# Broadcasting the decay rows of a state-space mixer: row layout in DRAM and the queue that loads them

## The chip, the cores and the metric

The kernel runs on one core of a Trainium2 chip. The metric is the device time of one execution in microseconds; the program is launched once and there is nothing to overlap it with. The engines are named as in the profile: PE (matrix multiplication), PEld (its weight loads), DVE (vector), ACT (scalar), POOL (GpSimd) and SP (the engine that does nothing here but issue DMAs). A DMA that SP or ACT issues goes through that engine's hardware queue; one that POOL issues goes through the software queue.

## The reference

One layer of a streaming encoder over 512 tokens of width 2048. A modulated RMS norm feeds one input projection, whose columns are split between two mixers; their outputs are projected, added to the input, and followed by a gated feed-forward with a short convolution. The change touches the second mixer only, the state-space one (four groups of four heads, chunks of tokens):

```python
dt = softplus(dt_raw + dt_bias)
a_head = -exp(a_log)
acum = cumsum(dt * a_head, within a chunk)            # one number per head and token
seg = exp(where(t >= s, acum[t] - acum[s], -inf))     # decay from token s to token t
cb = einsum('bctgn,bcsgn->bcgts', cm, bm)
y_diag = einsum('bcgts,bcgrts,bcsgrp->bctgrp', cb, seg, xdt)
```

For `seg` every partition (a token s) needs the whole row `acum[t]` of its head: a row of 512 numbers copied to all 128 partitions.

## The kernel before, in words

The weights stream through in chunks. `wchunk` has SP load two blocks of 128 rows into a `raw` tile (five buffers, shared with the tiles `m` of the modulation weights), ACT casts it to a high part `whi` (L161) and DVE subtracts to get the low part `wlo` (L162), two buffers each; PE multiplies each pair three times (L166 to L168). This runs from the start of the kernel to its end. Between the big matmuls, PE takes small steps of the two mixers: they are Python generators, advanced one step after every third big matmul by `small`, at most two at a time. Their matmuls write the two `mis` banks, so the third group in line waits until DVE or ACT has read the first.

`ssd_dt` computes the running sums `acum` for all 16 heads and four token blocks with one matmul into 64 rows (block-major, head inside), copies them to the SBUF tile `acr` (L398) and stores them to the DRAM tile `acrow` (L399). `ssd_mix(g)` handles a group of four heads; the groups run in pairs, 0 and 3, then 2 and 1. Its helper `decay(h)` loads the row of one head into a tile `mm` on all partitions (L434, sixteen loads in the kernel), adds the negative sums of the partition's own token (`negb`, L437), clips at zero (L439), takes the exponential on ACT (L440) and multiplies by the masked `cb` (L441). PE then multiplies `mm` by `xdt` (L487), DVE adds the result to `y` (L492), and PE makes the part that comes from earlier chunks (L497), which DVE scales and adds (L499, L503). At the end of `decay`, DVE has used the row and ACT the exponential; the next head's row is loaded while this head's matmuls run.

The `mm` tiles come from the pool of nine 2 KB-per-partition tiles that `T` hands out, in turn with all other temporaries. A scheduler (the tile framework) fixes the order of each engine's instructions when the program is built, and puts in the waits: a load waits for the last reader of its buffer, and hardware-queue loads take turns on eight semaphores, so that each also waits for the load that had its semaphore before.

In the background, `mod_unit` computes the modulation of later stages: SP loads a tile `m` (512 KB) between two weight chunks and DVE adds it into `macc` with two multiply-adds (L189). In the stretch of the state-space mixer every other weight chunk is followed by such a load.

Of the kernel before, what the change touches and what calls it, by code (L numbers as in the profile page):

```python
# [7 lines left out]
F32 = mybir.dt.float32  # L8
# [6 lines left out]
P = 128  # L15
S = 512
# [18 lines left out]
def hybrid_block_kernel(  # L35
# [6 lines left out]
    nc = tc.nc  # L42
# [22 lines left out]
    def T(name="t", dtype=F32):  # L65
        return tmp.tile([P, 512], dtype, tag="t", name=nm(name))
# [10 lines left out]
    def MIS(name="mis"):  # L77
        return psm.tile([P, 512], F32, tag="mis", name=nm(name))
# [4 lines left out]
    def CT(shape, name, dtype=F32):  # L83
        return cst.tile(shape, dtype, tag=name, name=name)
# [3 lines left out]
    def bc(ap, shape):  # L88
        return ap.unsqueeze(len(ap.shape)).broadcast_to(shape)
# [263 lines left out]
        A.activation(out=xbc[g][:, which, :], in_=y, func=AF.Silu)  # L353

    drm = ctx.enter_context(tc.tile_pool(name="drm", bufs=1, space=bass.MemoryType.DRAM))
    acrow = drm.tile([64, P], F32, tag="acrow", name="acrow")
    dtt = CT([P, 64], "dtt")
    dta = CT([P, 64], "dta")
    negb = CT([P, 16, 4, 2], "negb")
# [2 lines left out]
    def ssd_dt(src):  # L362
        pt = MIS()
        for t in range(NT):
            PE.transpose(out=pt[:, t * P:(t + 1) * P], in_=src[:, t * P:(t + 1) * P], identity=ident)
        xb, e, z, z2, p = (T(s_)[:, 0:64] for s_ in ("xb", "en", "zz", "z2", "pp"))

        def c4(t_):
            return t_.rearrange("p (c h) -> p c h", c=4)

        V.tensor_tensor(out=c4(xb), in0=c4(pt)[:, :, 0:16], in1=dtb.unsqueeze(1).broadcast_to([P, 4, 16]), op=ALU.add)
        V.tensor_tensor(out=c4(xb), in0=c4(pt)[:, :, 64:80], in1=c4(xb), op=ALU.add)
        V.scalar_tensor_tensor(out=e, in0=xb, scalar=-1.0, in1=xb, op0=ALU.mult, op1=ALU.min)
        A.activation(out=e, in_=e, func=AF.Exp)
        V.tensor_scalar(out=z, in0=e, scalar1=2.0, scalar2=None, op0=ALU.add)
        V.reciprocal(out=z, in_=z)
        V.tensor_tensor(out=z, in0=z, in1=e, op=ALU.mult)
        V.tensor_tensor(out=z2, in0=z, in1=z, op=ALU.mult)
        V.tensor_scalar(out=p, in0=z2, scalar1=1.0 / 19, scalar2=None, op0=ALU.mult)
        for k in (17, 15, 13, 11, 9, 7, 5, 3):  # L380
            V.scalar_tensor_tensor(out=p, in0=p, scalar=1.0 / k, in1=z2, op0=ALU.add, op1=ALU.mult)
        V.scalar_tensor_tensor(out=p, in0=p, scalar=1.0, in1=z, op0=ALU.add, op1=ALU.mult)
        V.tensor_scalar(out=xb, in0=xb, scalar1=0.0, scalar2=None, op0=ALU.max)
        V.scalar_tensor_tensor(out=dtt, in0=p, scalar=2.0, in1=xb, op0=ALU.mult, op1=ALU.add)
        V.tensor_tensor(out=c4(dta), in0=c4(dtt), in1=an.unsqueeze(1).broadcast_to([P, 4, 16]), op=ALU.mult)
        pc = MIS()
        for i, m in enumerate((tri, suf, ones, tri64, l1m)):
            PE.matmul(out=pc[:, i * 64:(i + 1) * 64], lhsT=m, rhs=dta, start=True, stop=True)
        A.activation(out=e3.rearrange("p a b -> p (a b)"), in_=pc[:, 0:192], func=AF.Exp)
        V.tensor_scalar(out=negb[:, :, :, 0].rearrange("p h c -> p c h"),  # L390
                        in0=pc[:, 192:256].rearrange("p (c h) -> p c h", h=16),
                        scalar1=-1.0, scalar2=None, op0=ALU.mult)
        V.tensor_copy(out=negb[:, :, :, 1].rearrange("p h c -> p c h"),
                      in_=pc[:, 256:320].rearrange("p (c h) -> p c h", h=16))
        pr = MIS()
        PE.matmul(out=pr[0:64, 0:P], lhsT=dta, rhs=tri64, start=True, stop=True)
        ar = T("acr")
        V.tensor_copy(out=ar[0:64, 0:P], in_=pr[0:64, 0:P])  # L398
        nc.gpsimd.dma_start(out=acrow, in_=ar[0:64, 0:P])  # L399

    def ssd_mix(g):

# [28 lines left out]
        def decay(h):  # L431
            hh = 4 * g + h
            m = mt[h] = T("mm")
            nc.gpsimd.dma_start(out=m.rearrange("p (c t) -> p c t", c=4),  # L434
                                in_=acrow.rearrange("(c h) t -> h c t", h=16)[hh].partition_broadcast(P))
            m8 = m.rearrange("p (a t) -> p a t", a=8)
            V.tensor_tensor(out=m8, in0=m8, in1=bc(negb[:, hh, :, :].rearrange("p c b -> p (c b)"), [P, 8, 64]),  # L437
                            op=ALU.add)
            V.tensor_scalar(out=m, in0=m, scalar1=0.0, scalar2=None, op0=ALU.min)  # L439
            A.activation(out=m, in_=m, func=AF.Exp)  # L440
            V.tensor_tensor(out=m, in0=m, in1=cbm, op=ALU.mult)  # L441

        decay(0)
        for cp in range(2):
            ps = MIS()
            for cc in range(2):
                for b in range(2):
                    t = 2 * cp + cc
# [33 lines left out]
        for h in range(4):  # L482
            if h < 3:
                decay(h + 1)
            ps = MIS()
            for cch in range(4):
                PE.matmul(out=ps[:, cch * HD:(cch + 1) * HD], lhsT=mt[h][:, cch * P:(cch + 1) * P],  # L487
                          rhs=xdt[:, cch, h * HD:(h + 1) * HD], start=True, stop=True)
                yield 0
            for cp in range(2):  # L490
                yh = ycols(cp)[:, :, h * HD:(h + 1) * HD]
                V.tensor_tensor(out=yh, in0=yh, in1=ps[:, cp * 128:(cp + 1) * 128].rearrange("p (t f) -> p t f", t=2),  # L492
                                op=ALU.add)
            if h < 3:
                ps = MIS()
                cch = h + 1
                PE.matmul(out=ps[:, 0:256], lhsT=xb[:, 3, cch * P:(cch + 1) * P], rhs=hst[h], start=True, stop=True)  # L497
                t = T("yo")[:, 0:256]
                V.tensor_tensor(out=t.rearrange("p (h f) -> p h f", h=4),  # L499
                                in0=ps[:, 0:256].rearrange("p (h f) -> p h f", h=4),  # L500
                                in1=bc(eac[:, cch, hs], [P, 4, HD]), op=ALU.mult)
                yo = yv(cch)[:, g * 256:(g + 1) * 256]
                V.tensor_tensor(out=yo, in0=yo, in1=t, op=ALU.add)  # L503
                yield 0
# [215 lines left out]
    for st, k0, k1 in SEGMENTS:  # L720
# [44 lines left out]
        if k1 == KT and st == 2:  # L765
            ssd_dt(dtraw)
# [52 lines left out]
    for j in range(2):  # L819
# [5 lines left out]
        for t in range(NT):  # L825
            sg = T("gs")
            A.activation(out=sg, in_=accs[t], func=AF.Silu)
            for i in range(4):
                h = 4 * j + i
# [208 lines left out]
```

## Time and profile before

| what | value |
|---|---|
| median of 3 runs | 2513.89 us (2510.45 to 2513.9) |
| the profiled execution | 2516.08 us |
| its span, first to last instruction | 2514.4 us |
| granted PE clock, mean over the span | 0.988 |
| DVE, ACT, POOL busy | 60%, 30%, 2% |
| the sixteen loads `mm<-acrow` | 256 KB each, issued from 287.6 to 437.9 us |

The span is 1.7 us shorter than the execution that it belongs to, and that execution lies 2.2 us above the median. The modulation and the first weight chunks fill the time to some 250 us, the state-space mixer runs beside the projection from about 290 to 460 us, the other mixer up to about 850 us, the output projection to 1060 us, and the feed-forward takes the rest. Times in the views of the profile count from the first instruction. "Busy" of PE includes modelled ends of matmuls, so what matters is where it was idle, how long, and what ended the idle time, and how fast its clock ran (the column PEclk, 1.00 being full speed).

### The profile page before, as it was taken

The numbers are of one execution on the slowest core, as the hardware profiler recorded it, in microseconds if no ns is written. First come the engines' busy times: TensorE is split into PE (matmuls) and PEld (weight loads), VectorE is DVE, ScalarE is ACT, GpSimd is POOL, SyncE is SP. The second block draws the span as 40 slices with busy tenths as digits, with TensorE's granted clock in tenths as the row PEclk, the third lists the DMA queues.
The fourth block names the chain that finished last, engine by engine and source line by source line (L and its number), as shares of the span: only waits on it lengthen the run. The fifth ranks groups of instructions, "written<-read, shape, count | busy, mean of one in ns | idle before, by whom it ended". The sixth has DMA issues, their size and how long they took to land.

```text
span 2514.4 us, 29234 instructions
## 1 busy us (share of the span) xinstructions
PE 2443.9 (97%) x11287; PEld 2015.4 (80%) x11287; DVE 1497.7 (60%) x2253; ACT 754.8 (30%) x1035; POOL 54.1 (2%) x66
## 2 busy tenths in 40 slices
PE   6999998999999999999999999999999999999998
PEld 5777877788878777887888888888888888888887
DVE  6884866556767656587636363635454545454557
ACT  6323422221322432332222222222222222232323
POOL 4000000000000000000000000000000000000000
PEclk8999999999999999999999999999999999999999
DMA  8893575335455666466323332333323232323242
GB/s 272 263 280 107 113 125 106 96 109 151 144 159 155 235 198 200 140 203 230 98 95 98 95 101 93 100 94 99 97 96 101 92 101 93 101 93 100 96 130 85
DMA packets 262823, 335.87 MB, mean 134 GB/s; under 512 B 18092, under 2 KB 182524, under 8 KB 261404
## 3 DMA queue, kind: packets, MB, share of 16 engines
q1 hardware_dynamic: 260432, 327.42, 41.5%
q0 software_dynamic: 1568, 4.31, 2.3%
q10 hardware_dynamic: 684, 2.28, 0.3%
q8 instruction: 88, 1.44, 0.2%
q14 instruction: 51, 0.42, 0.0%
HBM read 329.72 MB, written 4.23 MB: 133 GB/s over the span
## 4 chain that ended last, share of the span: by engine, by line
PE 81%; DMA 9%; DVE 7%; ACT 2%; issue 1%; SPq 0%; POOL 0%; ACTq 0%; DVEq 0%; POOLq 0%
PE acc L166 26%; PE acc L168 25%; PE acc L167 25%; DMA m<-in_w_mod_dram 7%; DVE wlo L162 2%; PE mis L547 2%; DVE macc L189 1%; DVE macc L238 1%; DMA raw<-in_w_in_dram 1%; ACT whi L161 1%; DMA x<-in_x_dram 1%; DMA mm<-acrow 0%; PE mis L201 0%; PE mis L487 0%; POOL rstd L265 0%
## 5 line engine op out<-in xcount | busy, mean ns | idle before, releaser
L162 DVE TENSOR_TENSOR wlo<-raw,whi 128x1024 fp32r<-128x1024 f32 (+1 forms) x408 | 490.4, 1203 | 744.9 <-ACT whi L161 739.3
L161 ACT CAST whi<-raw 128x1024 fp32r<-128x1024 f32 (+2 forms) x416 | 424.3, 1021 | 1403.3 <-PE acc L167 596.5
L166 PE MATMUL acc<-hhi,whi 128*128 128x512 f32 x1920 | 770.0, 402 | 11.7 <-ACT whi L161 7.1
L168 PE MATMUL acc<-hhi,wlo 128*128 128x512 f32 x1920 | 751.6, 394 | 3.6 <-DVE wlo L162 3.4
L167 PE MATMUL acc<-hlo,whi 128*128 128x512 f32 x1920 | 753.0, 392 | 0.0
L166 PEld LDWEIGHTS acc<-hhi,whi 128*128 128x128 f32 x1920 | 362.9, 189 | 87.2 <-ACT whi L161 11.2
L168 PEld LDWEIGHTS acc<-hhi,wlo 128*128 128x128 f32 x1920 | 362.4, 189 | 83.1 <-DVE wlo L162 6.5
L167 PEld LDWEIGHTS acc<-hlo,whi 128*128 128x128 f32 x1920 | 363.3, 189 | 67.9 <-issue 0.2
L166 PE MATMUL acc<-whi,act 128*128 128x512 f32 x640 | 249.0, 389 | 0.0
L167 PE MATMUL acc<-wlo,act 128*128 128x512 f32 x640 | 249.0, 389 | 0.0
L168 PE MATMUL acc<-whi,act 128*128 128x512 f32 x640 | 249.0, 389 | 0.0
L189 DVE SCALAR_TENSOR_TENSOR macc<-m,cT,macc 128x512 f32<-128x512 f32 x240 | 179.9, 750 | 106.8 <-DMA m<-in_w_mod_dram 102.6
L166 PE MATMUL acc<-whi,hhi 128*128 128x512 f32 x384 | 168.6, 439 | 0.0
L168 PE MATMUL acc<-whi,hlo 128*128 128x512 f32 x384 | 154.8, 404 | 0.0
L167 PE MATMUL acc<-wlo,hhi 128*128 128x512 f32 x384 | 154.0, 401 | 0.0
L166 PEld LDWEIGHTS acc<-whi,act 128*128 128x128 f32 x640 | 120.1, 188 | 25.0
L168 PEld LDWEIGHTS acc<-whi,act 128*128 128x128 f32 x640 | 120.1, 188 | 25.0
L167 PEld LDWEIGHTS acc<-wlo,act 128*128 128x128 f32 x640 | 120.1, 188 | 24.9
L950 DVE TENSOR_TENSOR g<-acc,gate 128x512 f32<-128x512 f32 x160 | 105.2, 683 | 3.9
L166 PE MATMUL acc<-mhi,whi 128*128 128x512 f32 x256 | 105.2, 411 | 0.0
L547 PEld LDWEIGHTS mis<-q,FK 128*128 128x128 f32 x448 | 83.5, 191 | 27.1 <-issue 8.3
L951 DVE TENSOR_TENSOR x<-x,g 128x512 f32<-128x512 f32 x160 | 105.1, 682 | 0.0
(263 smaller groups left out, 2249.8 us busy)
## 6 DMA issues: line engine op xcount, KB each, us to landing
raw<-in_ffn_w_up_dram SPq DMA_DIRECT2D x352, 256.0 KB, 2.9
m<-in_w_mod_dram SPq DMA_DIRECT2D x128, 512.0 KB, 4.3
raw<-in_ffn_w_down_dram SPq DMA_DIRECT2D x88, 512.0 KB, 3.6
m<-in_w_mod_dram SPq DMA_DIRECT2D x128, 256.0 KB, 4.3
raw<-in_w_in_dram SPq DMA_DIRECT2D x96, 256.0 KB, 3.5
raw<-in_w_in_dram SPq DMA_DIRECT2D x48, 512.0 KB, 3.8
raw<-in_w_out_dram SPq DMA_DIRECT2D x32, 512.0 KB, 4.6
x<-in_x_dram SPq DMA_DIRECT2D x8, 1024.0 KB, 10.6
```

Source lines behind the costliest of these rows:

```text
L161: A.copy(out=h_, in_=r_)
L162: V.tensor_tensor(out=l_, in0=r_, in1=h_.bitcast(F32), op=ALU.subtract)
L166: PE.matmul(out=ps, lhsT=lh, rhs=rh, start=first, stop=False)
L167: PE.matmul(out=ps, lhsT=lh, rhs=rl, start=False, stop=False)
L168: PE.matmul(out=ps, lhsT=ll, rhs=rh, start=False, stop=last)
L189: V.scalar_tensor_tensor(out=acc, in0=last[:, k, :], scalar=cT[:, kt:kt + 1], in1=acc, op0=ALU.mult, op1=ALU.add)
L238: V.scalar_tensor_tensor(out=acc, in0=m[:, k, :], scalar=cT[:, kt:kt + 1], in1=acc, op0=ALU.mult, op1=ALU.add)
L547: PE.matmul(out=ps[:, cch * 64:(cch + 1) * 64], lhsT=k[:, cch * P:(cch + 1) * P], rhs=qv[:, cch * npc:(cch + 1) * npc, 1, :], start=True, ...
L950: V.tensor_tensor(out=m, in0=accs[t], in1=gates[5][:, cs], op=ALU.mult)
L951: V.tensor_tensor(out=x1[t][:, cs], in0=x1[t][:, cs], in1=m, op=ALU.add)
```

## The change

Three lines. The DRAM tile becomes one row of 512 numbers (2 KB) per head; the store (still POOL's) scatters the 64 rows of 512 bytes to their places; and each broadcast reads one contiguous row and is issued by ACT on its hardware queue rather than by POOL on the software queue.

```diff
-    acrow = drm.tile([64, P], F32, tag="acrow", name="acrow")
+    acrow = drm.tile([16, S], F32, tag="acrow", name="acrow")
...
-        nc.gpsimd.dma_start(out=acrow, in_=ar[0:64, 0:P])
+        nc.gpsimd.dma_start(out=acrow.rearrange("h (c t) -> c h t", c=4), in_=ar[0:64, 0:P])
...
-            nc.gpsimd.dma_start(out=m.rearrange("p (c t) -> p c t", c=4),
-                                in_=acrow.rearrange("(c h) t -> h c t", h=16)[hh].partition_broadcast(P))
+            nc.scalar.dma_start(out=m, in_=acrow[hh].partition_broadcast(P))
```

The changed file is a line shorter, so everything behind L434 has a number lower by one there (L437 is L436, and so on). SP's instructions stand in the same order as before. ACT gets sixteen more rows, POOL loses sixteen, and on DVE and PE the scheduler moves instructions of the mixer by a few places. Three such places follow; numbers behind a name tell buffers apart.

ACT where the first pair of groups begins: `cy` and `xbc` belong to the short convolution, `whi` is the cast of a weight chunk. Before:

```order
L353 ACTIVATE xbc_126<-cy_2423 128x512
L349 ACTIVATE cy_2430<-xbc_126,p_663 128x512
L161 CAST whi_2633<-raw_2632 128x1024
L353 ACTIVATE xbc_126<-cy_2430 128x512
L440 ACT_TABLE_LOAD
L440 ACTIVATE mm_2495<-mm_2495 128x512
```

and now:

```order
L353 ACTIVATE xbc_126<-cy_2423 128x512
L349 ACTIVATE cy_2430<-xbc_126,p_663 128x512
L434 DMA mm_2495<-acrow 128x512
L434 DMA mm_2508<-acrow 128x512
L434 DMA mm_2694<-acrow 128x512
L161 CAST whi_2633<-raw_2632 128x1024
L434 DMA mm_2707<-acrow 128x512
L353 ACTIVATE xbc_126<-cy_2430 128x512
```

The first four broadcasts stand behind the last-but-one step of the convolution, and three of them ahead of a weight cast.

ACT at the last pair's end, where `q` belongs to the other mixer's first heads. Before:

```order
L522 ACTIVATE q_3292<-acc_2871 128x512
L161 CAST whi_3434<-raw_3433 128x1024
L440 ACT_TABLE_LOAD
L440 ACTIVATE mm_3337<-mm_3337 128x512
L440 ACTIVATE mm_3348<-mm_3348 128x512
L161 CAST whi_3485<-raw_3484 128x1024
L440 ACTIVATE mm_3414<-mm_3414 128x512
L440 ACTIVATE mm_3425<-mm_3425 128x512
```

and now:

```order
L521 ACTIVATE q_3292<-acc_2871 128x512
L434 DMA mm_3337<-acrow 128x512
L434 DMA mm_3348<-acrow 128x512
L161 CAST whi_3434<-raw_3433 128x1024
L439 ACT_TABLE_LOAD
L439 ACTIVATE mm_3337<-mm_3337 128x512
L439 ACTIVATE mm_3348<-mm_3348 128x512
L434 DMA mm_3414<-acrow 128x512
L161 CAST whi_3485<-raw_3484 128x1024
L434 DMA mm_3425<-acrow 128x512
L439 ACTIVATE mm_3414<-mm_3414 128x512
L439 ACTIVATE mm_3425<-mm_3425 128x512
```

Both weight casts now stand behind broadcasts, and each of these four broadcasts waits, on ACT, for the last reader of its buffer: mm_3337 and mm_3414 for matmuls of L487, mm_3348 and mm_3425 for additions of L503.

DVE in the first pair, where `y` is what a `mis` bank is emptied into. Before:

```order
L189 SCALAR_TENSOR_TENSOR macc_2931<-m_3019,cT,macc_2931 128x512 x2
L437 TENSOR_TENSOR mm_2768<-mm_2768,negb 128x512
L437 TENSOR_TENSOR mm_2779<-mm_2779,negb 128x512
L162 TENSOR_TENSOR wlo_2874<-raw_2872,whi_2873 128x1024
L439 TENSOR_SCALAR mm_2768<-mm_2768 128x512
L439 TENSOR_SCALAR mm_2779<-mm_2779 128x512
L492 TENSOR_TENSOR y_2449<-y_2449,mis_2774 128x2x64
L492 TENSOR_TENSOR y_2450<-y_2450,mis_2774 128x2x64
```

and now:

```order
L189 SCALAR_TENSOR_TENSOR macc_2931<-m_3019,cT,macc_2931 128x512
L436 TENSOR_TENSOR mm_2768<-mm_2768,negb 128x512
L189 SCALAR_TENSOR_TENSOR macc_2931<-m_3019,cT,macc_2931 128x512
L438 TENSOR_SCALAR mm_2768<-mm_2768 128x512
L436 TENSOR_TENSOR mm_2779<-mm_2779,negb 128x512
L162 TENSOR_TENSOR wlo_2874<-raw_2872,whi_2873 128x1024
L440 TENSOR_TENSOR mm_2768<-mm_2768,cbm_2493 128x512
L438 TENSOR_SCALAR mm_2779<-mm_2779 128x512
L491 TENSOR_TENSOR y_2449<-y_2449,mis_2774 128x2x64
L491 TENSOR_TENSOR y_2450<-y_2450,mis_2774 128x2x64
```

One multiplication by the mask moved ahead of the two additions that empty the bank; on PE, the matmul that waits for this bank (L497 into mis_2822) moved behind three more big matmuls.

## The prediction

> **What bounds the kernel now.** I read the page's totals first, then the stretches, then what ended PE's idle time, then the chain of waits through those places.
>
> ```profile
> span 2514.4 us, 29234 instructions
> PE 2443.9 (97%) x11287; PEld 2015.4 (80%) x11287; DVE 1497.7 (60%) x2253; ACT 754.8 (30%) x1035; POOL 54.1 (2%) x66
> 260.00:330.00 70.00, 69.74 (x328) 57.06 (x327) 61.67 (x96) 33.68 (x45) 4.37 (x6) 1.00 0.58 116
> 330.00:460.00 130.00, 115.72 (x551) 94.51 (x550) 78.92 (x155) 31.96 (x41) 8.21 (x11) 0.93 0.59 112
> 460.00:590.00 130.00, 129.83 (x694) 108.61 (x694) 78.74 (x160) 29.67 (x54) 2.05 (x2) 1.00 0.38 110
> ```
>
> PE bounds the kernel. The last three rows are stretches: start and end, length, then busy time of PE, PEld, DVE, ACT and POOL, the granted PE clock, the DMA share and GB/s. Eleven of the sixteen broadcasts are issued in the middle one, and there alone PE is idle, 14.3 us of 130, and its clock falls to 0.93, 9 us lost at most. The stretch after it, with as much DVE work, loses nothing: that is the floor to be reached. POOL's 2% says that issuing costs it nothing that matters; what a broadcast does elsewhere is the question.
>
> ```profile
> PE mis L497 <- DVE y L492: 11.8, 3, 4.4
> PE mis L449 <- DVE cbm L427: 2.2, 1, 2.2
> 345.00 0.40 PE L168 MATMUL acc<-whi,hlo 128*128 128x512 f32 x1
> 349.27 0.67 PE L497 MATMUL mis<-xbc 128*128 128x256 f32 x2 [3.87 <-DVE y L492]
> 380.53 0.33 PE L449 MATMUL mis<-ident,xbc 128*128 128x128 f32 x1 [2.21 <-DVE cbm L427]
> 433.60 2.05 PE L497 MATMUL mis<-xbc 128*128 128x256 f32 x4 [4.37 <-DVE y L492]
> 448.77 0.89 PE L497 MATMUL mis<-xbc 128*128 128x256 f32 x2 [3.56 <-DVE y L492]
> ```
>
> So the 14.0 us are four gaps, and each ends when DVE has emptied a bank. Why is DVE late? The chain of waits (start, length, what):
>
> ```profile
> 335.58 8.57 DMA m<-in_w_mod_dram
> 344.18 0.76 DVE macc L189
> 345.63 1.29 DVE mm L437 x2
> 346.92 1.14 DVE wlo L162
> 348.06 0.67 DVE mm L439 x2
> 348.73 0.41 DVE y L492 x2
> 371.78 6.53 DMA m<-in_w_mod_dram
> 379.79 0.70 DVE cbm L427
> 419.33 9.16 DMA m<-in_w_mod_dram
> 437.94 8.63 DMA mm<-acrow
> ```
>
> Ahead of gaps 1 to 3 DVE stands in its queue at `macc`, waiting for a modulation tile that takes 6.5 to 9.2 us; behind it stand the weight split and the additions that PE needs. Gap 4 is a broadcast itself. The DMA view says how unusual this is; the first two rows are from 330 to 460 us, the next two from 480 to 730, the rest from the page.
>
> ```profile
> m<-in_w_mod_dram SPq DMA_DIRECT2D x7, 512.0 KB, 5.6
> mm<-acrow POOLq DMA_DIRECT2D x11, 256.0 KB, 9.2
> m<-in_w_mod_dram SPq DMA_DIRECT2D x34, 512.0 KB, 3.7
> raw<-in_w_in_dram SPq DMA_DIRECT2D x24, 256.0 KB, 3.4
> gate<-in_b_mod_dram ACTq DMA_DIRECT2D x1, 1024.0 KB, 4.7
> q0 software_dynamic: 1568, 4.31, 2.3%
> q10 hardware_dynamic: 684, 2.28, 0.3%
> ```
>
> The last column of the first five is the median from issue to landing. A modulation tile takes 3.7 us where no broadcast runs.
>
> **The change, part by part.**
>
> *One broadcast.* The page's queue rows (packets, MB, share of 16 engines' span) give the software queue 2.3% of 16 x 2514 us, 925 engine-us for 4.31 MB, or 54 for one broadcast: 3.4 us of all sixteen engines. ACT's hardware queue, whose bytes are mostly `gate`, also a broadcast to 128 partitions, took 121 for 2.28 MB: 13 for a broadcast, 0.8 us of all sixteen. From issue to landing the ends are 3.4 us (a plain load of 256 KB) and 9.2 (as now); I take 3.5, since `gate` moved four times the bytes by this queue in 4.7. Broadcasts of 2 KB rows are not in the trace, only `gate`'s of 8 KB; per byte they would have to cost four times as much to be where the software queue is.
>
> The Trainium skill speaks against this: its page "DMA: Bandwidth & Descriptors" (section "Issuing engines are not separate DMA queues") says that DMAs of ACT, SP and POOL run on the same 16 engines and interleave, and that another issuer saves only issue time. By it the modulation tiles would stay late; that is rival B, and the two queue rows, 54 against 13, speak against reading it so here.
>
> *Gap 1.* The tile issued at 335.58 now has two broadcasts just ahead of it (they stand behind the cast `whi` whose split frees this tile's buffer), so 3.7 + 2 x 0.8 = 5.3: it lands at 340.9. In DVE's new order come two `macc` (0.7 each), two L437 (0.6 each), one L439 (0.3), the split (1.14), one L441 (0.6 like L437), one L439 and two L492 (0.4 together): 5.4, so the bank is free at 346.3. PE used to run dry at 345.4; three big matmuls (0.4 each, overlapping) moved ahead of the waiting one make it 346.1. I leave 0.5 of 3.87, to be safe.
>
> *Gap 2.* No broadcast is in flight at 371.78 any more: the second pair's first four now stand behind the cast below. 3.7 rather than 6.53 us puts the bank 2.8 us earlier, more than the gap of 2.2. Nothing is left.
>
> *Gap 3.* 419.33 + 3.7 + 0.8 for the broadcast just ahead of it = 423.8; two `macc` 1.5, split 1.1, two L437 1.2, two L439 0.7, L492 0.4: 428.7, before PE ran dry at 429.2. Nothing left.
>
> *Gap 4.* The last broadcast went at 437.94, when L503 had freed its buffer. Without gap 3 (4.4) and the slow clock up to there (1.4) that is 432.1, and it lands at 435.6 to 436; L437, L441, L439 and L492 take 2, to 438. PE, earlier by gap 3 and all of its slow clock (4.4 + 2.6), would run dry at 445.2 - 7.0 = 438.2. I leave 0.3.
>
> *Clock.* The clock is the third column from the end; the stretch cut at the gaps reads:
>
> ```profile
> 330.00:370.00 40.00, 36.13 (x181) 30.08 (x180) 25.34 (x55) 9.73 (x14) 5.22 (x7) 0.96 0.76 119
> 370.00:410.00 40.00, 37.77 (x177) 29.64 (x175) 28.51 (x44) 10.22 (x13) 0.00 (x0) 0.96 0.41 112
> 410.00:450.00 40.00, 31.81 (x149) 26.37 (x150) 19.76 (x44) 9.02 (x12) 2.99 (x4) 0.90 0.66 105
> ```
>
> Gaps 1 and 2 each lose 0.04 x 40 = 1.6 us of clock, gap 3 up to 4.0, and the rest of the 9 (0.07 x 130 for the whole stretch) falls behind gap 4. Some of it lay in idle time, so I take 8.
>
> *ACT.* The timeline around the moved loads, and `gate`'s issue:
>
> ```profile
> 287.64 0.80 POOL L434 DMA_DIRECT2D mm<-acrow  x1 [25.96 <-ACT xbc L353]
> 307.92 0.82 ACT L349 ACTIVATE cy<-xbc,p 128x512 f32<-128x512 f32 x1
> 310.91 0.69 DVE L437 TENSOR_TENSOR mm<-mm,negb 128x512 f32<-128x512 f32 x1
> 376.29 1.05 ACT L161 CAST whi<-raw 128x1024 fp32r<-128x1024 f32 x1 [5.79 <-PE acc L167]
> 382.13 0.68 DVE L437 TENSOR_TENSOR mm<-mm,negb 128x512 f32<-128x512 f32 x1
> 421.06 0.75 POOL L434 DMA_DIRECT2D mm<-acrow  x1 [2.25 <-DVE y L503]
> 423.29 1.05 ACT L161 CAST whi<-raw 128x1024 fp32r<-128x1024 f32 x1 [6.18 <-PE acc L167]
> 1058.01 0.39 ACTq L257 DMA_DIRECT2D gate<-in_b_mod_dram  x1
> ```
>
> Sixteen issues of 0.39 each are 6 us of an engine that is 30% busy; what it costs is place. POOL issued the first at 287.6; on ACT it stands behind the L349 that starts at 307.92, so it goes at about 308.4 (the issue at 1058.01 ran beside an activation) and lands at 311.9, where DVE wants it at 310.91: a wait of 1.0, with the weight split and the mixer's `xdt` behind it, on the engine that is busy 61.7 of 70 us there. PE has no idle time there to hide it in, but a weight chunk in hand: 0 to 1.3, I take 0.7. The second pair's four go at 377.4, behind the cast of 376.29, and land from 380.9, before DVE's 382.13. The waits that ACT now makes are short: the one for L503 ended at 421.06 and the cast behind it is not ready before 423.29. SP's loads now also wait for broadcasts that had their semaphore before, but each of these goes some 9 us earlier or more.
>
> *The store* goes out in 64 pieces of 512 bytes rather than in one run; it had landed before POOL's first broadcast at 287.64, and its first reader now comes 20 us later: nothing. *POOL* loses sixteen issues that nothing waited for: nothing.
>
> *Sum.* Idle 14.0 - 0.8 = 13.2, clock 8, start -0.7: 20.5, say 20. The profiled execution took 2516.1 (its span 2514.4 and 1.7 around it), which gives 2496; it lay 2.2 above the median of the runs, so against that median, 2513.9, I forecast 2494.
>
> **Rivals.**
>
> A. Part of the gaps stays. Gap 1 and gap 4 close with nothing to spare above. If a broadcast ahead of a modulation tile costs it 2 us rather than 0.8, gaps 1 and 3 keep 2.0 and 1.5, each with its half-speed window (1.6 and 2.6): 0.5 is already left, so 7.2 less than 20 is won, 12.8, 2501. For it: DMA shares of 0.76 and 0.66 in two of the rows above, so that queues are long. Against it: 13 engine-us. The Trainium skill's "TensorE: Matmul & The Clock Gate" (section "What's actually happening") has the clock halve after an idle window of about 3.4 us; by that, such gaps would cost no clock, and A would be 2497. The trace differs: behind gap 2, 2.21 us, the clock fell to 0.96.
>
> B. The bytes are what holds the engines, and ACT's issuing changes only the landing. Then gaps 1 to 3 stay, gap 4 (3.6, and 1.6 of clock) goes, 0.7 is lost at the start: 4.5 won, 2509.
>
> C. Slower: reading one 2 KB row 128 times is what takes 9.2 us, in either layout and queue. Then the late issue bites: the first broadcast lands at 317.6, DVE stands 6.7 us at 310.91 and PE, with a chunk in hand but the `mis` banks behind DVE, loses about 6 and 2.5 of clock; the second pair's lands at 386.6, 4.5 after DVE wants it, of which 2 reach PE; gap 2 still goes (2.2 and 1.6). 10.5 lost less 3.8, 6.7: 2521. It decides from a landing of some 6 us on. Against it: `gate`.
>
> **How the numbers follow.** My forecast 0.62, A 0.20, B 0.08, C 0.06, and 0.04 for a loss elsewhere that eats the gain, 2509 to 2520. The forecast's own range is 2490 (all four gaps, 9 of clock, no loss at the start) to 2499. With A (2496 to 2505) and part of B, the range 2489 to 2508 leaves out C, the losses and most of B, 0.17. What this measurement can tell from no change is 0.2%, 5 us: faster than 2508.9 are the forecast, A and half of B, 0.86; within it the other half of B and half of the losses, 0.06; slower C and the other half, 0.08.
>
> **What would show it.** Right: `mm` landing in 3 to 4 us; `m` between 330 and 440 us near 4; the waits of L497 and L449 for DVE under 2 us in total; a PE clock of 1.00 there; POOL's queue with some 0.1% of the engines. Wrong in size: DVE waiting for `mm` at the start of a pair by more than 1.5 us (place on ACT), or `m` still above 5.5 (A, B). Wrong in kind: PE waiting for `whi`, which would mean that ACT stood at a broadcast with a weight cast behind it.

## The result, and the profile after

The changed kernel takes 2499.39 us, median of 4 runs (2497.71 to 2500.41), against 2513.89 (2510.45 to 2516.95) before: a ratio of 0.9942, with a 95% interval of 0.9925 to 0.9959. That is 14.5 us less; 20 were forecast. The time lies inside the forecast's range and on the forecast's side, 5.4 us above the 2494 that was forecast. The profiled execution took 2500.41.

First the page's totals, its rows of the two queues, and the first two stretches that were shown of before (the columns are the same).

```profile
span 2498.7 us, 29189 instructions
PE 2435.8 (97%) x11287; PEld 2008.5 (80%) x11287; DVE 1498.6 (60%) x2253; ACT 755.3 (30%) x1035; POOL 42.3 (2%) x50
q10 hardware_dynamic: 2988, 6.47, 0.9%
q0 software_dynamic: 304, 0.12, 0.0%
260.00:330.00 70.00, 68.18 (x322) 55.86 (x321) 59.47 (x91) 33.27 (x44) 0.68 (x1) 1.00 0.37 112
330.00:460.00 130.00, 126.70 (x642) 104.80 (x641) 88.21 (x169) 36.25 (x46) 0.00 (x0) 0.99 0.42 124
```

PE's idle time in the long stretch went from 14.3 to 3.3 us, and the clock from 0.93 to 0.99; in the stretch ahead of it, 1.6 us were lost. The DMA share fell from 0.59 to 0.42, although more bytes were moved (124 GB/s, 112 before). The rest of what was idle is in three gaps:

```profile
PE mis L448 <- DVE y L455: 4.0, 2, 2.4
PE mis L496 <- DVE y L491: 0.7, 1, 0.7
317.48 0.63 PE L448 MATMUL mis<-ident,xbc 128*128 128x128 f32 x4 [1.55 <-DVE y L455]
348.88 0.67 PE L496 MATMUL mis<-xbc 128*128 128x256 f32 x2 [0.72 <-DVE y L491]
387.42 0.41 PE L448 MATMUL mis<-ident,xbc 128*128 128x128 f32 x2 [2.43 <-DVE y L455]
```

The gap at 349 is what is left of gap 1. Those at 317 and 387 are new: they stand where a pair of groups begins. The loads and the chain of waits through these places say why:

```profile
m<-in_w_mod_dram SPq DMA_DIRECT2D x8, 512.0 KB, 3.7
mm<-acrow ACTq DMA_DIRECT2D x12, 256.0 KB, 4.7
309.31 4.55 DMA mm<-acrow
337.67 5.63 DMA m<-in_w_mod_dram
375.31 8.31 DMA mm<-acrow
```

The modulation tiles (330 to 460 us, median to landing) are back at 3.7 us. Broadcasts land in 4.7, not 3.5, and the last of a bunch of four takes 8.31. ACT issued that bunch at one go, and DVE, which now arrives earlier, waited for three of the four (the last three rows; the row at 313.31 is DVE's wait at the start of the first pair):

```profile
308.44 1.31 ACTq L434 DMA_DIRECT2D mm<-acrow  x3
373.97 1.78 ACTq L434 DMA_DIRECT2D mm<-acrow  x4
313.31 0.69 DVE L436 TENSOR_TENSOR mm<-mm,negb 128x512 f32<-128x512 f32 x1 [1.79 <-DMA mm<-acrow]
377.61 0.69 DVE L436 TENSOR_TENSOR mm<-mm,negb 128x512 f32<-128x512 f32 x1 [0.58 <-DMA mm<-acrow]
379.64 0.69 DVE L436 TENSOR_TENSOR mm<-mm,negb 128x512 f32<-128x512 f32 x1 [0.89 <-DMA mm<-acrow]
383.64 0.69 DVE L436 TENSOR_TENSOR mm<-mm,negb 128x512 f32<-128x512 f32 x1 [1.52 <-DMA mm<-acrow]
```

Both new gaps are thus of the change's own making: the rows are asked for too late. What the trace cannot tell is which half of the change made the old gaps go, the layout of the rows or the queue.

### The profile page after: what moved, and what is told of

Read it like the earlier page. It is cut to its first block, busy times and chain, and to the rows that moved or that the text cites. A ratio compares the mean times of both kernels' runs of the same rounds, so it can differ in the third digit from the quotient of the medians.

```text
span 2498.7 us, 29189 instructions
## 1 busy us (share of the span) xinstructions
PE 2435.8 (97%) x11287; PEld 2008.5 (80%) x11287; DVE 1498.6 (60%) x2253; ACT 755.3 (30%) x1035; POOL 42.3 (2%) x50
## 4 chain that ended last, share of the span: by engine, by line
PE 84%; DMA 7%; DVE 6%; ACT 1%; issue 1%; POOL 0%; SPq 0%; ACTq 0%; DVEq 0%; POOLq 0%
PE acc L166 27%; PE acc L168 26%; PE acc L167 26%; DMA m<-in_w_mod_dram 6%; DVE wlo L162 2%; PE mis L546 2%; DVE macc L189 1%; DVE macc L238 1%; ACT whi L161 1%; DMA mm<-acrow 1%; PE mis L486 0%; DMA x<-in_x_dram 0%; DMA raw<-in_w_in_dram 0%; PE mis L852 0%; DMA raw<-in_ffn_w_up_dram 0%
```

## The experiments

The experiments ran in three batches, each on one chip beside runs of the kernel before. These took 2512.84 us (7 runs) beside the two halves, the held-back modulation loads and the plain rows; 2513.2 (11 runs) beside the three kernels on the place of the issue and the plain pieces on ACT's queue; and 2510.41 (1 run) beside the plain pieces on POOL's queue and the three kernels with padded rows. Runs of the kernel before spread from 2508 to 2517, so the time of a single run is worth some 4 us either way, and kernels that ran once are read by their profiles.

### Each half alone

The layout alone: the changed kernel, with its broadcasts on POOL.

```diff
-            nc.scalar.dma_start(out=m, in_=acrow[hh].partition_broadcast(P))
+            nc.gpsimd.dma_start(out=m, in_=acrow[hh].partition_broadcast(P))
```

> The new DRAM layout (2 KB rows) with POOL's software queue still broadcasting them. Theory Q (the software queue is what holds the DMA engines, 54 engine-us a broadcast, whatever the length of the pieces): queue 0 keeps about 2.3% of the engines, the broadcasts land after about 9 us, the modulation tiles between 330 and 460 us stay near 5.6 us, and the time stays within 4 us of the kernel before (2514). Theory L (the cost is by the piece, and four times fewer pieces cost a quarter): queue 0 falls to about 0.7%, the broadcasts land in 4 to 5 us, and since POOL issues them early, without ACT's order, the time is below the changed kernel's: 2490 to 2496.

The queue alone: the kernel before, with its broadcasts on ACT.

```diff
-            nc.gpsimd.dma_start(out=m.rearrange("p (c t) -> p c t", c=4),
+            nc.scalar.dma_start(out=m.rearrange("p (c t) -> p c t", c=4),
```

> The old DRAM layout (four pieces of 512 bytes to a row) broadcast by ACT's hardware queue. Theory Q: 512 pieces of 512 bytes at the 27 ns that this queue takes for such a piece are 14 engine-us, as many as 128 rows of 2 KB, so everything is as in the changed kernel: landing 3 to 8 us, 2497 to 2501. Theory L: the pieces cost the same as on the software queue, the modulation tiles stay late, and with the late issue on ACT the time is 2512 or more.

Measured: the layout alone 2493.76 us (2491.14 to 2495.51), ratio 0.992 [0.99, 0.9941]; the queue alone 2530.26 (2524.94 to 2533.17), ratio 1.0067 [1.0046, 1.0087]. From the profile of the layout alone, its software queue, the long stretch and its loads there:

```profile
q0 software_dynamic: 1584, 4.31, 0.6%
330.00:460.00 130.00, 129.38 (x665) 107.42 (x664) 90.89 (x174) 36.34 (x46) 6.02 (x11) 1.00 0.43 125
m<-in_w_mod_dram SPq DMA_DIRECT2D x8, 512.0 KB, 3.8
mm<-acrow POOLq DMA_DIRECT2D x11, 256.0 KB, 4.0
```

and of the queue alone the same rows, with its two waits of PE:

```profile
q10 hardware_dynamic: 9132, 6.47, 1.1%
330.00:460.00 130.00, 109.84 (x528) 89.64 (x526) 76.98 (x147) 29.51 (x38) 0.00 (x0) 0.91 0.39 104
m<-in_w_mod_dram SPq DMA_DIRECT2D x7, 512.0 KB, 8.0
mm<-acrow ACTq DMA_DIRECT2D x12, 256.0 KB, 9.4
PE mis L449 <- DVE y L456: 14.9, 2, 10.0
PE mis L497 <- DVE y L492: 10.1, 2, 5.8
```

The answer is plain. On the same software queue and with the same bytes, one 2 KB row instead of four pieces takes the queue's share from 2.3% to 0.6%, the landing from 9.2 to 4.0 us, and PE's idle time in the stretch from 14.3 to 0.6. With the old layout the hardware queue lands no sooner than the software queue did (9.4). ACT also asks later: it issues the second pair's four rows together, from 388.43 on, the last of them lands after 15.71 us, and a gap of 10 us opens behind them. Theory Q, the prediction's own, falls in both runs. The gain is the layout's; the queue costs.

### Is it the late modulation tile that holds PE?

The kernel before, with the modulation loads held back while the first pair of groups runs (`rate` is what lets them in; the first is back at 380 us).

```diff
-        rate[0] = 0.5
+        rate[0] = 0.5 if pr else 0
```

> The kernel before, with the background loads of modulation tiles held back until the first pair of heads of the other mixer is done (they follow later; all is computed). Theory M (PE's gaps 1 to 3 are DVE standing at a late modulation tile, with the banks that PE needs behind it): the gaps of 3.9, 2.2 and 4.4 us are gone or under 1 us each, the one of 3.6 us, which is a broadcast's own, stays, and PE's idle time between 330 and 460 us falls from 14.3 to about 4. Theory W (the late broadcasts themselves hold DVE up, the tiles only happen to be in front): at least three gaps stay, and the idle time is above 9 us.

One run: 2498.75 us. The long stretch, and of the chain and of PE's gaps:

```profile
330.00:460.00 130.00, 122.24 (x610) 100.98 (x608) 81.31 (x157) 34.33 (x45) 8.21 (x11) 0.97 0.56 103
409.92 8.66 DMA m<-in_w_mod_dram
427.19 8.62 DMA mm<-acrow
423.69 1.21 PE L497 MATMUL mis<-xbc 128*128 128x256 f32 x4 [3.88 <-DVE y L492]
438.01 1.00 PE L497 MATMUL mis<-xbc 128*128 128x256 f32 x2 [3.61 <-DVE y L492]
```

Gaps 1 and 2 are gone, though the broadcasts were nearly as slow as before (8.6 us in the median, 9.2 before). Gap 3 stays, since the modulation loads were back by then and one took 8.66, and so does gap 4, where the broadcast itself is what DVE waits for. For that reason PE's idle time is 7.8 us, between theory M's 4 and theory W's 9. Holding the loads back also took their multiply-adds out of DVE's way, two of some 0.75 us for a tile, which is less than either gap. So the chain of the prediction holds for gaps 1 and 2: a slow broadcast hurts by the modulation tile that it delays and for which DVE stands, and PE behind DVE. Gap 3, with a late tile in front of it again, fits it.

### Why do the rows land late in the changed kernel: the same row 128 times, or the bunch?

The changed kernel, with each partition reading a 2 KB piece of its own weight row, so that the decays are not computed from the layer's sums.

```diff
-            nc.scalar.dma_start(out=m, in_=acrow[hh].partition_broadcast(P))
+            nc.scalar.dma_start(out=m, in_=wup[hh * P:(hh + 1) * P, 0:512])
```

> The changed kernel, its sixteen loads reading 128 different rows of 2 KB from a weight matrix in place of one row 128 times (so the mixer's decays are wrong numbers; all the rest is done as before). Theory B (the landing of 5 to 8 us where several loads go together is the sum of the bytes that stand in the engines' queues): landings as in the changed kernel, 3.3 us alone and 7 to 8.5 us for the last of four, median 4.5 to 5.2. Theory H (reading one row 128 times is slow): all land within 3.3 to 4.5 us, the packets' mean falls from 115 ns to about 85, and the gap of 2.4 us near 385 us is gone.

One run: 2493.88 us.

```profile
mm<-in_ffn_w_up_dram ACTq DMA_DIRECT2D x12, 256.0 KB, 3.3
```

The median falls from 4.7 to 3.3 us and the gaps at the start of the two pairs from 1.55 and 2.43 to 0.6 and 0.5; the last of the bunch of four still takes 6.4, where theory H asked for 4.5 at most and theory B for 7 or more. Both have a part: between these two profiles, reading one row 128 times costs 1.4 us in the median and 1.9 for the last of the bunch, and bunching makes the rest.

### Does the place on ACT cost what remains?

The changed kernel and the layout alone once more, five runs each, beside six of a third: the changed kernel with the first two heads of each group on POOL and the other two on ACT.

```diff
-            nc.scalar.dma_start(out=m, in_=acrow[hh].partition_broadcast(P))
+            q = nc.gpsimd if h < 2 else nc.scalar
+            q.dma_start(out=m, in_=acrow[hh].partition_broadcast(P))
```

> The changed kernel once more, on the chip and in the rounds of the next two, so that the three can be set side by side: 2497 to 2501, 0.994 of the kernel before by either theory.

> The new layout alone (POOL still issues) once more, beside the changed kernel. If the early issue by POOL is worth what the trace says (no gaps of 1.6, 0.7 and 2.4 us and no half-speed window of 1.7 lost), it is 5 to 7 us below the changed kernel of the same rounds; if the difference seen was between chips or rounds, it is within 2 us of it.

> The new layout; the rows of the first two heads of each group (the eight that ACT issues in two bunches of four) go by POOL, the other eight stay on ACT's hardware queue. Theory P (the changed kernel's new gaps come from the place of the issue: late and four at once behind a weight cast on ACT): the gaps of 1.6 us near 316 and 2.4 us near 385 are gone, 0.7 near 348 may stay, and the time is 2493 to 2496, level with the layout alone. Theory S (the software queue itself is better for a broadcast): it falls half way between the two, 2496 to 2498, and the loads on ACT's queue land later than those on POOL's, 5 us and more.

| kernel | us (lowest to highest) | ratio to before |
|---|---|---|
| changed | 2497.82 (2495.77 to 2501.57) | 0.9943 [0.9931, 0.9955] |
| layout alone, POOL | 2493.59 (2491.43 to 2494.18) | 0.9921 [0.9908, 0.9934] |
| rows shared by POOL and ACT | 2494.13 (2488.67 to 2498.38) | 0.9924 [0.9911, 0.9937] |

No run of the layout alone is as slow as the fastest of the changed kernel; the medians are 4.2 us apart, a little less than the 5 to 7 expected. The kernel with shared rows has both queues in one profile (330 to 460 us):

```profile
mm<-acrow ACTq DMA_DIRECT2D x8, 256.0 KB, 3.8
mm<-acrow POOLq DMA_DIRECT2D x4, 256.0 KB, 3.9
260.00:330.00 70.00, 69.74 (x328) 57.20 (x328) 61.82 (x97) 33.63 (x45) 2.88 (x5) 1.00 0.37 112
```

A broadcast lands as fast by one queue as by the other here. With the first two rows of a group on the idle engine the start has no gap (69.74 of 70 us busy, 68.18 in the changed kernel), and the one of 2.43 us is gone too: PE's longest wait for DVE is 0.8 us. What the move to ACT costs is place: POOL, which has nothing else in its queue in this stretch, issued the second pair's rows some 20 us before ACT's 373.97. In the layout alone:

```profile
351.29 0.55 POOL L434 DMA_DIRECT2D mm<-acrow  x1 [7.65 <-PE mis L486]
354.15 1.15 POOL L434 DMA_DIRECT2D mm<-acrow  x2 [2.31 <-DVE mm L440]
355.76 0.55 POOL L434 DMA_DIRECT2D mm<-acrow  x1 [0.46 <-DVE y L491]
```

### What about the old layout is slow?

Two kernels take the old form, four 512-byte pieces per partition, but read pieces of 128 different weight rows, 2 KB apart in each. First the kernel of the queue alone with this edit, then the kernel before:

```diff
-                                in_=acrow.rearrange("(c h) t -> h c t", h=16)[hh].partition_broadcast(P))
+                                in_=wup[hh * P:(hh + 1) * P, 0:2048].rearrange("p (c r) -> p c r", c=4)[:, :, 0:P])
```

> ACT's hardware queue with four pieces of 512 bytes to a partition, as in the run that took the new queue with the old layout (2530 us, landing 9.4 us), but read from 512 different places of a weight matrix, not from four places 128 times each (so the mixer's decays are wrong numbers). Theory D (the price is by the piece: 512 descriptors rather than 128, wherever they read): the loads land after 8 to 10 us as there, the modulation tiles between 330 and 460 us take about 8, the time is 2525 to 2535. Theory H (the price is 128 readers of the same 512 bytes of DRAM): they land in 3.3 to 6.5 us like the plain rows of 2 KB, the tiles in 3.7 to 4.5, and the time is 2492 to 2498.

> The kernel before, on POOL's software queue with its 512-byte pieces, but each partition reads its own four places of a weight matrix rather than the four of the decay row (the decay values are therefore other numbers, of the same amount of work). Theory H (the price is that 128 partitions read the same four places): a broadcast lands in 3.5 to 5 us, the software queue's share falls from 2.3% to about 0.7%, gaps stay under 1 us in all, time about 2494. Rival D (512-byte pieces on the software queue are dear by themselves): landing about 9, gaps 1 to 4 all there, time about 2513.

One run each: 2495.01 us on ACT's queue and 2487.74 on POOL's. The loads of the first, and of the second the queue and the loads:

```profile
mm<-in_ffn_w_up_dram ACTq DMA_DIRECT2D x12, 256.0 KB, 4.2
q0 software_dynamic: 1568, 4.31, 0.6%
mm<-in_ffn_w_up_dram POOLq DMA_DIRECT2D x11, 256.0 KB, 3.6
```

They land in 4.2 us on ACT's queue, against 9.4 with the decay row's pieces, and in 3.6 on POOL's, against 9.2. So the number of pieces is not it. At that point I took the repeated reading of four places to be the cause. But these two kernels had changed the distance between the pieces as well, 2 KB where it had been 8 KB (sixteen heads of 512 bytes). The last three runs keep the repeated reading and change the distance: a head's pieces 640 bytes apart on ACT's queue, 10 KB apart on ACT's, and 640 bytes apart on POOL's. The first, against the kernel of the queue alone (the third is the same against the kernel before):

```diff
-    acrow = drm.tile([64, P], F32, tag="acrow", name="acrow")
+    acrow = drm.tile([16, 4, 160], F32, tag="acrow", name="acrow")
...
-        nc.gpsimd.dma_start(out=acrow, in_=ar[0:64, 0:P])
+        nc.gpsimd.dma_start(out=acrow[:, :, 0:P].rearrange("h c t -> c h t"), in_=ar[0:64, 0:P])
...
-                                in_=acrow.rearrange("(c h) t -> h c t", h=16)[hh].partition_broadcast(P))
+                                in_=acrow[hh, :, 0:P].partition_broadcast(P))
```

The second, also against the queue alone, keeps the order of the rows and pads each to 640 bytes:

```diff
-    acrow = drm.tile([64, P], F32, tag="acrow", name="acrow")
+    acrow = drm.tile([64, 160], F32, tag="acrow", name="acrow")
...
-        nc.gpsimd.dma_start(out=acrow, in_=ar[0:64, 0:P])
+        nc.gpsimd.dma_start(out=acrow[:, 0:P], in_=ar[0:64, 0:P])
...
-                                in_=acrow.rearrange("(c h) t -> h c t", h=16)[hh].partition_broadcast(P))
+                                in_=acrow.rearrange("(c h) t -> h c t", h=16)[hh][:, 0:P].partition_broadcast(P))
```

> As the run with the old layout on ACT's queue, but a head's four 512-byte pieces stand 640 bytes apart in DRAM rather than 8 KB (too far apart to be read as one run of 2 KB). Theory N (many small reads of one place are what is slow): landing about 9 us as at 8 KB, time about 2530. Rival K (it is the step of 8 KB): landing 4 to 5 us as with the 2 KB rows, gaps of 3 to 5 us in all, time about 2498.

> As before this one, but block-major again, with rows of 640 bytes: a head's four pieces stand 10 KB apart, so the step is no longer a power of two. Theory N: landing about 9, time about 2530. Rival K, if what matters is a power of two: landing 4 to 5, about 2498; if what matters is that the pieces are far apart: about 9, as N, but then the pieces 640 bytes apart land in 4 to 5.

> The kernel before with POOL's queue, and a head's four pieces 640 bytes apart. Theory N: landing about 9, the software queue at about 2.3%, gaps as before, time about 2513. Rival K: landing about 4, the queue at about 0.7%, time about 2494.

One run each: 2493.36, 2497.4 and 2495.17 us. Their loads in the stretch, in that order, and the last one's queue:

```profile
mm<-acrow ACTq DMA_DIRECT2D x12, 256.0 KB, 4.4
```

```profile
mm<-acrow ACTq DMA_DIRECT2D x12, 256.0 KB, 4.5
```

```profile
q0 software_dynamic: 1584, 4.31, 0.7%
mm<-acrow POOLq DMA_DIRECT2D x11, 256.0 KB, 4.5
```

The theory of repeated small reads, which I had favoured, asked for 9 us in all three and falls. The same 512-byte pieces, read just as often, land in 4.5 us at a step of 640 bytes or of 10 KB, and in 9.4 at 8 KB. Far apart is not it either. What the old layout had wrong is the step of 8 KB, as far as these runs separate it: the third kernel keeps POOL's queue and the number of pieces, and lands its rows in 4.5 us where the kernel before took 9.2.

The Trainium skill has a related rule ("DMA: Bandwidth & Descriptors", section "Latency and other measured facts"): copies between DRAM tensors are slow when the pitch from one partition's row to the next is a large power of two, and some KB of padding restore them. There the slow pitches are 2 MB and more, and 512 KB is still close to the full rate. Here the step lies between four pieces that every partition reads, 8 KB is enough, and 2 KB more (10 KB) restore the landing.

Three things stay open. Each padded kernel ran once. Padding to 640 bytes also moved where pieces begin within 512 bytes and how far apart the rows of different heads lie, which no run separates from the step. And rows that differ from partition to partition were never read at a step of 8 KB, so whether the step needs the repeated reading to be slow wasn't tried. (The weight pieces at a step of 2 KB, a power of two as well, were not slow. The weight rows of the plain-row run lie 45,056 bytes apart, so that every second one is a multiple of 8 KB from the first, and landed in 3.3 us.)

## Why the prediction was right in the main, and where it was wrong

**The chain was right.** Modulation tiles late by the broadcasts, DVE standing at `macc`, PE behind DVE, gap 4 a broadcast itself: the run with the modulation loads held back shows it for gaps 1, 2 and 4. Gaps 3 and 4 went as worked out. Gap 1: the tile took 5.63 us where 5.3 was worked out, and 0.72 is left where 0.5 was.

**"One broadcast" named the wrong cause for the right size.** It set 54 engine-us on the software queue against 13 on ACT's and gave the difference to the queue. But `gate`, from which the 13 came, differs in queue and in layout. (It is about half of that queue's 2.28 MB, not most; the rest is nearly all another broadcast of an 8 KB row, `fnb`. And 256 KB are 0.262 of the page's MB, which makes the two prices 56 and 14. Nothing hangs on either.) The layout alone brings the software queue down to 0.6%, 0.006 x 16 x 2493.8 = 239 engine-us or 15 a broadcast, and the old layout on ACT's queue lands in 9.4. On that queue it even takes little engine time: 0.011 x 16 x 2529.6 = 445 engine-us less the 121 of the queue's other loads, some 20 a broadcast where POOL's took 54, and the modulation tiles took 8.0 us beside it. So engine time, by which the prediction judged what a broadcast does to a tile, does not decide how late the tile is: in the changed kernel it is some 15 a broadcast, and the tiles took 3.7 us. The Trainium skill's rule that DMAs of all issuers share the same engines ("DMA: Bandwidth & Descriptors", section "Issuing engines are not separate DMA queues"), which the prediction set aside, agrees with the landings: 9.2 us by POOL and 9.4 by ACT in the old layout, 3.9 and 3.8 in the new. Rival B's price, 2509, did not come. Rival C was right that a landing of 9 us on ACT's queue loses (the queue alone: 17 us slower), but it held this landing to come with any layout, and with the new one it does not.

**How far this was luck.** The change as a whole was priced about right because `gate` differs from the old broadcasts in both halves at once. For the queue alone the same reasoning gave 2497 to 2501 (theory Q), and it measured 2530.

**By the prediction's own signs** it was wrong in size: DVE waited 1.79 and 1.52 us for a row at the start of a pair, above the 1.5 named there (place on ACT), and L448 and L496 waited 4.7 us for DVE instead of under 2. The tiles (3.7 us), POOL's queue (0.0%) and nearly the clock (0.99) came as forecast, and PE did not wait for `whi`. The time lies at the upper end of the forecast's own range, 2490 to 2499, and within rival A's, but not for A's reason: gap 3 is gone and only 0.72 us is left of gap 1.

**The landing of 3.5 us was too low.** It measured 4.7 in the median, 8.31 for the last of four in a bunch beside SP's loads.

**The start** was put at 0.7 us of loss and measured 1.6: the rows went at 308.44, as worked out (308.4), but the first that DVE needed landed at 313.3, not 311.9.

**"Nothing is left" of gap 2 was wrong.** The rows were to land "before DVE's 382.13". That time was itself late by the wait that the change takes away (6.58 us for a modulation tile). In the changed kernel DVE was there at 377.0 (the wait of 0.58 before 377.61), 1.3 to 3 us after the rows were issued, and a new gap of 2.43 us opened, with a clock of 0.96 in its 40 us:

```profile
378.34 1.54 DVE L189 SCALAR_TENSOR_TENSOR macc<-m,cT,macc 128x512 f32<-128x512 f32 x2 [6.58 <-DMA m<-in_w_mod_dram]
```

```profile
370.00:410.00 40.00, 37.43 (x176) 29.68 (x175) 28.98 (x47) 9.72 (x12) 0.00 (x0) 0.96 0.47 133
```

The first row is of before, the second of after.

**The sum.** Idle time in the stretch: 13.2 forecast, 14.3 - 3.3 = 11.0 measured. Start: -0.7 and -1.6. Clock: 8, and what is left of the profiled difference, 2516.1 - 2500.4 - 11.0 + 1.6 = 6.3. Together 15.7 between the two profiled executions, 14.5 between the medians. (The clock's own rows give 0.07 x 130 = 9.1 before and 0.04 x 40 = 1.6 after, a difference of 7.5; the 1.2 by which the two differ lie elsewhere in the kernel and were not followed up.) Without the place on ACT, the layout alone comes to 2493.6, where the forecast had put the whole change. So the terms that were too small are the landing and the wait for ACT's place, the new gaps of 1.6 and 2.43 us and the clock behind the second.

## What to carry to other kernels

When a load is slow, look at the addresses it reads before you look at the queue that carries it, and where a change has two halves, price and run each alone: here one was worth 19 us and the other cost 4. An issue moved from an idle engine to a busy, in-order one goes out when that engine gets there, late and in bunches; and the time at which a consumer "wants" its data must be read after the wait that the change removes. Of the versions that compute the layer and ran more than once, the layout alone, with the broadcasts left on POOL, has the lowest median (2493.6), level with the rows shared by POOL and ACT (2494.1).

## What the hardware showed that I had not expected

- Four 512-byte pieces 8 KB apart, read by all 128 partitions, land in 9.2 us (POOL) and 9.4 (ACT); 640 bytes or 10 KB apart in 4.4 to 4.5. Beside the slow ones a 512 KB load of another queue took 5.6 us (POOL) and 8.0 (ACT) in the median, instead of 3.7.
- On ACT's queue that slowness hardly shows in the queue's share of the engines: 1.1% at a step of 8 KB, 0.9% at 10 KB, with landings of 9.4 and 4.5. Nor does it in the DMA share of the stretch: 0.39 with the slow rows on ACT's queue, 0.42 in the changed kernel. The share of busy time is no guide to how late a transfer is.
- The 2.43 us gap cost clock (0.96 in its row above). Those of 1.55 and 0.72 did not: the stretch of the first has 1.00, and so has the piece that holds the second (the row below). In the second batch a gap of 1.66 us at the same place in the changed kernel left the clock at 1.00.

```profile
330.00:370.00 40.00, 39.27 (x205) 32.66 (x204) 28.55 (x61) 11.08 (x15) 0.00 (x0) 1.00 0.43 125
```
